# A Conformer-like layer: wg and wu by seven products of quadrants, the ffn in four blocks

## The chip, the cores and the metric

One core of a Trainium2 chip runs the whole layer. The metric is device time in microseconds. Engines in play: PE (TensorE, matmuls; PEld is its loading of weights), DVE (VectorE), ACT (ScalarE), POOL (GpSimd), and SP, which issues the DMAs.

## The reference, cut to what matters

512 tokens, 1024 features, 2816 ffn columns (22 tiles of 128). The layer has a feed-forward (ffn1), a mixer of three attentions, and a second feed-forward (ffn2). Only the two feed-forwards are touched by the change.

```python
def swiglu(h, wg, wu, wd):
    return (jax.nn.silu(h @ wg) * (h @ wu)) @ wd

x = x + 0.5 * swiglu(rmsnorm(x, ffn1_norm[l]), ffn1_wg[l], ffn1_wu[l], ffn1_wd[l])
...
x = x + 0.5 * swiglu(rmsnorm(x, ffn2_norm[l]), ffn2_wg[l], ffn2_wu[l], ffn2_wd[l])
x = rmsnorm(x, final_norm[l])
```

## The kernel before, in words

Every operand of a large product is split into a high and a low part of 12 significant bits (`split`, lines 72 to 75: ACT casts the high part, DVE subtracts it for the low part), and `mm3` (lines 105 to 109) makes three matmuls of each pair: high by high, high by low, low by high.

An ffn (`ffn`, from line 242) first has the normalised tokens in transposed form: `rows_T` and `norm_T` take one tile of 128 tokens at a time, scale it on DVE (line 138), transpose it on PE (line 146) into a PSUM bank `ps_t`, and split it from there into `hh` and `hl` (8 feature tiles by 512 tokens). For each of the 22 tiles of ffn columns, 128 columns of wg and of wu are loaded (`wraw`, 512 KB each), split into `whi` and `wlo` (128 x 1024), and multiplied: 8 feature tiles, three matmuls each, 512 tokens wide (`up_mm`). The gate's bank goes through silu on ACT (line 261), DVE multiplies it with the up product (line 263, tile `pr`), and the result is split into `gh` and `gl`. The first two tiles of each ffn take the tokens in two parts of 256, since the norms of the later tokens are not there yet.

After 11 tiles, `add_product` (line 200) multiplies `gh`, `gl` with the rows of wd in two halves of 512 output columns and adds to `x_sb` on DVE (line 230); then the other 11 tiles follow. Chunks of weights rotate through 5 raw buffers (line 70) and 4 split ones (line 98). In the mixer an order for PE is written out by hand; elsewhere a scheduler orders each engine's instructions by its own estimate of time. ffn2's tokens come from the product with w_out, row tile by row tile (`row_ffn`, tile `norms`).

## Time and profile before

| | us |
|---|---|
| median of 3 runs | 1302.09 (1301.76 to 1302.15) |
| span of the profiled execution | 1299.5 |
| PE busy in it | 1284.3 (99%) |
| DVE busy | 591.0 (45%) |
| ACT busy | 476.7 (37%) |
| POOL busy | 105.3 (8%) |

ffn1 lies from the start to about 390 us, ffn2 from about 920 us to the end. A busy PE only says that some matmul was under way; what one costs is read from the distance between the starts of two.

### The profile page before, as it was taken

The page shows a single profiled execution, that of the slowest core. Times are in us where ns is not written, and L with a number is a line of the kernel's source. Part 1 is how long each engine was busy: PE and PEld are TensorE (multiplying, and loading weights), DVE is VectorE, ACT ScalarE, POOL GpSimd, SP SyncE. Part 2 cuts the span into 40 slices and gives each one's busy share as a digit, 9 for nine tenths or more (in the row PEclk, how much of TensorE's full clock was granted, in tenths as well). Part 3 has the DMA queues.
Part 4 walks back from the last instruction along what each step waited for, and adds up shares of the span by engine and source line. Part 5 has one row for each costly group of instructions (what it writes and reads, how often), then busy time and mean ns, then how long its engine had stood idle before and what let it go on. Part 6 is the DMA issues. An engine that isn't in the chain of part 4 may idle for free.

```text
span 1299.5 us, 16334 instructions
## 1 busy us (share of the span) xinstructions
PE 1284.3 (99%) x6416; PEld 1089.5 (84%) x6416; DVE 591.0 (45%) x1067; ACT 476.7 (37%) x923; POOL 105.3 (8%) x110
## 2 busy tenths in 40 slices
PE   8999999999999999999999999999999999999997
PEld 7888888888888799999999998888888888888886
DVE  5433324333256666766666465454433322333322
ACT  4422213222234446554555454342332211322222
POOL 2000000000000201111122021110000000000010
PEclk8999999999999999999999999999999999999999
DMA  7432233222254403221232121264133223332221
GB/s 266 127 98 89 85 102 113 91 89 89 73 178 139 116 25 107 85 85 50 85 102 75 52 86 49 74 202 162 31 116 98 79 84 97 114 98 90 81 73 65
DMA packets 53132, 127.35 MB, mean 98 GB/s; under 512 B 10176, under 2 KB 10688, under 8 KB 53056
## 3 DMA queue, kind: packets, MB, share of 16 engines
q1 hardware_dynamic: 52480, 125.27, 30.3%
q8 instruction: 50, 0.82, 0.3%
q10 hardware_dynamic: 576, 1.05, 0.2%
q14 instruction: 26, 0.21, 0.1%
HBM read 122.11 MB, written 4.19 MB: 97 GB/s over the span
## 4 chain that ended last, share of the span: by engine, by line
PE 97%; ACT 1%; DVE 1%; DMA 0%; issue 0%; POOL 0%; SPq 0%; POOLq 0%; ACTq 0%; DVEq 0%
PE ps_g L107 12%; PE ps_g L108 12%; PE ps_g L109 12%; PE ps_s L109 7%; PE ps_s L108 7%; PE ps_s L107 7%; PE ps_p L107 7%; PE ps_p L109 7%; PE ps_p L108 7%; PE ps_o L109 3%; PE ps_o L108 3%; PE ps_o L107 3%; PE ps_o L641 2%; PE ps_s L609 2%; PE ps_t L457 1%; PE ps_t L146 1%
## 5 line engine op out<-in xcount | busy, mean ns | idle before, releaser
L74 ACT CAST whi<-wraw 128x1024 fp32r<-128x1024 f32 (+2 forms) x176 | 173.5, 991 | 508.2 <-issue 180.8
L75 DVE TENSOR_TENSOR wlo<-wraw,whi 128x1024 fp32r<-128x1024 f32 (+1 forms) x174 | 199.7, 1151 | 293.8 <-ACT whi L74 288.1
L107 PE MATMUL ps_g<-hh,whi 128*128 128x512 f32 (+1 forms) x288 | 106.4, 370 | 0.8 <-ACT hh L74 0.8
L108 PE MATMUL ps_g<-hl,whi 128*128 128x512 f32 (+1 forms) x288 | 106.6, 370 | 0.0
L109 PE MATMUL ps_g<-hh,wlo 128*128 128x512 f32 (+1 forms) x288 | 106.4, 370 | 0.0
L107 PE MATMUL ps_p<-whi,hh 128*128 128x384 f32 (+1 forms) x264 | 95.2, 360 | 0.0
L107 PE MATMUL ps_s<-hh,whi 128*128 128x512 f32 (+1 forms) x240 | 92.2, 384 | 0.0
L108 PE MATMUL ps_s<-hl,whi 128*128 128x512 f32 (+1 forms) x240 | 92.1, 384 | 0.0
L109 PE MATMUL ps_s<-hh,wlo 128*128 128x512 f32 (+1 forms) x240 | 91.6, 382 | 0.0
L109 PE MATMUL ps_p<-whi,hl 128*128 128x384 f32 (+1 forms) x264 | 89.5, 339 | 0.0
L108 PE MATMUL ps_p<-wlo,hh 128*128 128x384 f32 (+1 forms) x264 | 89.4, 339 | 0.0
L107 PE MATMUL ps_g<-hh,fh 128*128 128x512 f32 x192 | 77.9, 406 | 0.0
L109 PE MATMUL ps_g<-hh,fl 128*128 128x512 f32 x192 | 75.1, 391 | 0.0
L108 PE MATMUL ps_g<-hl,fh 128*128 128x512 f32 x192 | 75.0, 391 | 0.0
L118 POOL TENSOR_TENSOR rsh<-msh,mhalf 128x4 f32<-128x4 f32 x38 | 42.9, 1129 | 262.3 <-DVE msh L124 202.8
L107 PEld LDWEIGHTS ps_g<-hh,whi 128*128 128x128 f32 x288 | 54.1, 188 | 10.9 <-ACT hh L74 1.0
L108 PEld LDWEIGHTS ps_g<-hl,whi 128*128 128x128 f32 x288 | 54.2, 188 | 9.9
L109 PEld LDWEIGHTS ps_g<-hh,wlo 128*128 128x128 f32 x288 | 54.2, 188 | 9.9
L75 DVE TENSOR_TENSOR fl<-wraw,fh 128x768 fp32r<-128x768 f32 x48 | 48.8, 1017 | 26.3 <-ACT fh L74 26.2
L108 PEld LDWEIGHTS ps_s<-hl,whi 128*128 128x128 f32 x240 | 45.8, 191 | 9.4 <-DVE hl L75 0.2
L107 PEld LDWEIGHTS ps_s<-hh,whi 128*128 128x128 f32 x240 | 46.0, 192 | 9.1
L74 ACT CAST fh<-wraw 128x768 fp32r<-128x768 f32 x48 | 39.8, 832 | 37.1 <-PE ps_g L108 22.0
(294 smaller groups left out, 2783.3 us busy)
## 6 DMA issues: line engine op xcount, KB each, us to landing
wraw<-in_ffn_w SPq DMA_DIRECT2D x88, 512.0 KB, 3.5
wraw<-in_ffn_wd SPq DMA_DIRECT2D x40, 512.0 KB, 3.6
wraw<-in_w_u SPq DMA_DIRECT2D x32, 384.0 KB, 3.1
wraw<-in_w_gb SPq DMA_DIRECT2D x32, 384.0 KB, 3.1
wraw<-in_w_gf SPq DMA_DIRECT2D x16, 384.0 KB, 3.1
wraw<-in_w_mem_kv SPq DMA_DIRECT2D x8, 512.0 KB, 4.8
wraw<-in_w_out SPq DMA_DIRECT2D x8, 512.0 KB, 4.1
x_sb<-in_x SPq DMA_DIRECT2D x4, 512.0 KB, 7.1
```

Source lines behind the costliest of these rows:

```text
L74: nc.scalar.copy(out=hi, in_=raw)
L75: (engine or nc.vector).tensor_tensor(out=lo, in0=raw, in1=f32(hi), op=ALU.subtract)
L107: nc.tensor.matmul(ps, lhsT=st[0], rhs=mv[0], start=first, stop=False)
L108: nc.tensor.matmul(ps, lhsT=st[0], rhs=mv[1], start=False, stop=False)
L109: return nc.tensor.matmul(ps, lhsT=st[1], rhs=mv[0], start=False, stop=last)
L118: nc.gpsimd.tensor_tensor(out=rs, in0=ms, in1=mhalf[:, :n], op=ALU.pow)
L146: nc.tensor.transpose(ps[:, k * P:(k + 1) * P], xn[:, c:c + P], ident)
L457: nc.tensor.transpose(ps[:, j * P:(j + 1) * P], pt[:, j * P:(j + 1) * P], ident)
L609: nc.tensor.matmul(out_, lhsT=q, rhs=k, start=j == 0, stop=j == 1)
L641: nc.tensor.matmul(o[:, vs], lhsT=pT[:, j * P:(j + 1) * P], rhs=un.v[:, j, vs], start=j == 0, stop=j == i)
```

## The change

Both operands of h wg and h wu are cut into quadrants: the features into two halves of 512, the tokens into two halves of 256, and the ffn columns into pairs of tiles. The product of such a pair, 2 x 2 quadrants by 2 x 2, is made by seven products instead of eight (Winograd's form of Strassen's method), each half as many tokens wide.

- On the side of the tokens seven operands M1 to M7 (`mhi`, `mlo`) are made once for each ffn. With r0, r1 the two halves of the features and lo, hi the tokens' halves: M1 = r0 lo, M2 = r1 lo, M3 = r1 hi, M5 = t1 = r0 hi - r0 lo, M6 = t2 = r1 hi - t1, M7 = t3 = r1 hi - r0 hi, M4 = t4 = r1 lo - t2. The transposed rows are first copied by ACT into raw tiles; the differences and the splits follow (`Operands`).
- On the side of the weights each pair of tiles (`Item`) loads four raw chunks, as before, which are now quadrants with wg and wu side by side. Four sums s1 to s4 (tiles `quarter`) are made on DVE, and seven blocks are split instead of four: `whi`/`wlo` and, in the feed-forward's own pool, `fhi`/`flo`, a ring of six.
- One product is 24 matmuls of 256 columns (`mm7`): gate and up, four feature tiles, three terms. Products 1, 6, 7 and 4 accumulate in one bank, which ACT copies out between them (`snap`); products 5 and 3 in another; DVE adds the copies (`plus`) and the gating works on halves of the tokens (`gated`).
- The ffn goes in four blocks of 4, 6, 6 and 6 tiles, each followed by its part of the product with wd; a list of jobs gives PE's order, and weights are prepared up to six blocks ahead. The first four products of an ffn need only the first two token tiles.
- Raw buffers become 6. The memory rows' norm is issued before ffn1's last half product instead of between its halves; pools move from the mixer's to one that lasts longer.

Comments were removed as well. The core of the diff, empty lines left out:

```diff
+CHUNKS = (4, 6, 6, 6)
+HS = S // 2
...
-        return base.tile([P, 1024], F32, tag="raw", name=name, bufs=5)
+        return base.tile([P, 1024], F32, tag="raw", name=name, bufs=6)
...
+    def new_M(pool):
+        mh, ml = (pool.tile([P, 7, 4, HS], F32R, name=n) for n in ("mhi", "mlo"))
+        return {i: (mh[:, i - 1], ml[:, i - 1]) for i in range(1, 8)}
+    quarters = [0]
+    def quarter():
+        quarters[0] += 1
+        return base.tile([P, 1024], F32, tag=("w4", "kx")[quarters[0] % 2], name="quarter", bufs=2)
...
+        def rows(self, src, ss, gain, t):
+            ms = tiny("ms", 1)
+            nc.vector.tensor_scalar(out=ms, in0=ss[:, 0:1], scalar1=EPS, scalar2=ss[:, 1:2], op0=ALU.add, op1=ALU.add)
+            rs = rsqrt(ms)
+            xn = scratch("xn")
+            for dh in range(2):
+                norm_half(xn, src, rs, gain, dh)
+                ps = bank("t")
+                for k in range(4):
+                    c = (dh * 4 + k) * P
+                    nc.tensor.transpose(ps[:, k * P:(k + 1) * P], xn[:, c:c + P], ident)
+                nc.scalar.copy(out=self.raw[dh][:, :, t * P:(t + 1) * P], in_=k4(ps))
+            self.combine(t)
+        def combine(self, t):
+            M, (r0, r1) = self.M, self.raw
+            sub = nc.vector.tensor_tensor
+            cols, first = slice(t * P, (t + 1) * P), slice(t % 2 * P, (t % 2 + 1) * P)
+            def part(i, raw, c):
+                split(raw, M[i][0][:, :, c], M[i][1][:, :, c])
+            if t < 2:
+                part(1, r0[:, :, cols], cols)
+                part(2, r1[:, :, cols], cols)
+                return
+            if t == 2:
+                self.t1, self.t2 = k4(quarter()), k4(quarter())
+            t1, t2 = self.t1, self.t2
+            sub(out=t1[:, :, first], in0=r0[:, :, cols], in1=r0[:, :, first], op=ALU.subtract)
+            sub(out=t2[:, :, first], in0=r1[:, :, cols], in1=t1[:, :, first], op=ALU.subtract)
+            part(6, t2[:, :, first], first)
+            if t == 3:
+                lo, hi = slice(0, HS), slice(HS, S)
+                split(t1, *M[5])
+                t3, t4 = k4(quarter()), k4(quarter())
+                sub(out=t3, in0=r1[:, :, hi], in1=r0[:, :, hi], op=ALU.subtract)
+                split(t3, *M[7])
+                sub(out=t4, in0=r1[:, :, lo], in1=t2, op=ALU.subtract)
+                split(t4, *M[4])
+                split(r1[:, :, hi], *M[3])
...
+    def run_jobs(jobs, ring):
+        made = alive = 0
+        for n, job in enumerate(jobs):
+            while made < len(jobs) and (made <= n or alive + jobs[made].blocks <= ring):
+                alive += jobs[made].blocks
+                jobs[made].got = jobs[made].prep() if jobs[made].prep else None
+                made += 1
+            with tc.manual_schedule(engines={mybir.EngineType.PE}):
+                job.run(job.got)
+            alive -= job.blocks
...
-        hh, hl = h
-        nf = NF // 2
-                def up_mm(ps, w, c0, c1):
-                    for k in range(ND):
-                        o = slice(k * P, (k + 1) * P)
-                        mm3(ps[:, c0:c1], (w[0][:, o], w[1][:, o]), (hh[:, k, c0:c1], hl[:, k, c0:c1]),
-                            k == 0, k == ND - 1)
...
-                    # the first tiles take the tokens in two parts, as their norms come in
-                    for c0, c1 in [(0, 256), (256, 512)] if group == 2 else [(0, 512)]:
-                        for i in range(group):
-                            for j in range(2):
-                                up_mm(pss[i][j], ws[i][j], c0, c1)
...
+        RING = 6
+        spot = [0]
+        def block(raw):
+            spot[0] += 1
+            if spot[0] % RING < 4:
+                return weight(None, 1024, raw=raw)
+            return weight(None, 1024, fp, ("fhi", "flo"), RING - 4, raw=raw)
+        def mm7(ps, blk, m, first):
+            for j in range(2):
+                c = slice(j * HS, (j + 1) * HS)
+                for k in range(4):
+                    o = slice((j * 4 + k) * P, (j * 4 + k + 1) * P)
+                    st, mv = tuple(w[:, o] for w in blk), tuple(v[:, k, :] for v in M[m])
+                    for n, (x, y) in enumerate(((st[0], mv[0]), (st[0], mv[1]), (st[1], mv[0]))):
+                        nc.tensor.matmul(ps[:, c], lhsT=x, rhs=y, start=first and j + k + n == 0,
+                                         stop=k == 3 and n == 2, skip_group_check=True)
...
+            def prep(self, p):
+                add = nc.vector.tensor_tensor
+                if p == 1:
+                    return block(self.raw(0))
+                if p == 2:
+                    return block(self.raw(1))
+                if p == 6:
+                    self.s1, self.s2 = quarter(), quarter()
+                    add(out=self.s1, in0=self.raw(2), in1=self.raw(3), op=ALU.add)
+                    add(out=self.s2, in0=self.s1, in1=self.raw(0), op=ALU.subtract)
+                    return block(self.s2)
+                if p == 5:
+                    got = block(self.s1)
+                    self.s4 = quarter()
+                    add(out=self.s4, in0=self.raw(1), in1=self.s2, op=ALU.subtract)
+                    return got
+                if p == 7:
+                    s3 = quarter()
+                    add(out=s3, in0=self.raw(0), in1=self.raw(2), op=ALU.subtract)
+                    return block(s3)
+                if p == 4:
+                    return block(self.raw(3))
+                return block(self.s4)
...
+            def run(self, p, blk):
+                if p == 1:
+                    self.y = bank("s")
+                    mm7(self.y, blk, 1, True)
+                    self.p1 = self.snap()
+                elif p == 2:
+                    x = bank("g")
+                    mm7(x, blk, 2, True)
+                    self.gated(self.plus(x, self.p1), 0, 0)
+                elif p == 6:
+                    mm7(self.y, blk, 6, False)
+                    self.u2 = self.snap()
+                elif p == 5:
+                    self.z = bank("p" if self.ft // 2 % 2 else "o")
+                    mm7(self.z, blk, 5, True)
+                elif p == 7:
+                    mm7(self.y, blk, 7, False)
+                    self.u3 = self.snap()
+                    self.gated(self.plus(self.z, self.u3), 1, 1)
+                elif p == 4:
+                    mm7(self.y, blk, 4, False)
+                    self.gated(self.y, 1, 0)
+                    self.done(1)
+                else:
+                    mm7(self.z, blk, 3, False)
+                    self.gated(self.plus(self.z, self.u2), 0, 1)
+                    self.done(0)
...
+            order = []
+            if ft == 0:
+                order += [(items[0], 1), (items[0], 2), (items[1], 1), (items[1], 2)]
+            else:
+                order += [(items[0], 1), (items[0], 2)]
+            for i, item in enumerate(items):
+                order += [(item, 6), (item, 5), (item, 7)]
+                if i + 1 < len(items) and not (ft == 0 and i == 0):
+                    order += [(items[i + 1], 1)]
+                if ft == 0 and i == 0:
+                    order += [(item, 4), (item, 3)]
+                elif i + 1 < len(items):
+                    order += [(item, 4), (item, 3), (items[i + 1], 2)]
+            jobs = [product(*o) for o in order]
+            end = [product(items[-1], 4), product(items[-1], 3)]
...
+                    for k in range(0, nf, 2):
+                        jobs.append(Job(lambda k=k, chunk=chunk: chunk(k), lambda wc, k=k, run=run: run(wc, k)))
+                        if dh == 0 and k == 0:
+                            jobs += end
...
+    ops = Operands(M1, new_G_as_raw(fp))
+    for t in range(NT):
+        ops.rows(x_sb[:, t, :], squares(x_sb[:, t, :]), gain1, t)
...
+    Mp = right_pool("M2")
+    rawp = right_pool("raw2")
+    M2 = new_M(Mp.__enter__())
+    rp = rawp.__enter__()
+    ops = Operands(M2, [rp.tile([P, 4, S], F32, name=n) for n in ("raw0", "raw1")])
...
-        w = w.reshape(2, ND, P, NF, P).transpose(3, 0, 2, 1, 4)       # ft, g/u, p, k, f
+        w = np.stack([f[pre + "_wg"][0], f[pre + "_wu"][0]])
+        w = w.reshape(2, 2, 4, P, NF, P).transpose(4, 1, 3, 0, 2, 5)
```

How instructions stand in the rows. On PE, inside an ffn, before, where the product for wg (bank `ps_p`) ends and that for wu (bank `ps_o`) begins:

```order
L108 MATMUL ps_p<-hl,whi 128x512
L109 MATMUL ps_p<-hh,wlo 128x512
L107 MATMUL ps_o<-hh,whi 128x512
L108 MATMUL ps_o<-hl,whi 128x512
L109 MATMUL ps_o<-hh,wlo 128x512
```

And now, where product 5 (bank `ps_o`) is broken off for product 6 (bank `ps_s`):

```order
L354 MATMUL ps_o<-mlo,fhi 128x256
L354 MATMUL ps_o<-mhi,flo 128x256
L354 MATMUL ps_o<-mhi,fhi 128x256
L354 MATMUL ps_s<-mhi,whi 128x256
L354 MATMUL ps_s<-mlo,whi 128x256
L354 MATMUL ps_s<-mhi,wlo 128x256
```

The triples of terms stay, with 256 columns in place of 512, and seven groups of 24 stand for two tiles where four groups of 24 stood.

On DVE at the start of ffn1, before, after the norms of the token tiles (`hl` is the low part of the transposed rows, `mt` a row tile of the memory, `wlo` that of a weight chunk, `pr` the first gated product):

```order
L75 TENSOR_TENSOR wlo<-wraw,whi 128x1024
L75 TENSOR_TENSOR hl<-ps_t,hh 128x4x128 x4
L153 TENSOR_SCALAR ms<-ss 128x1
L138 SCALAR_TENSOR_TENSOR xn<-mt,rs,gain 128x512 x2
L75 TENSOR_TENSOR wlo<-wraw,whi 128x1024
L263 TENSOR_TENSOR pr<-sg,ps_s 128x512
```

And now, where the last operands M are made (`gl` is here the memory of r1; L379 makes s1, L380 s2, L402 is `plus`), up to the low part of s1's block:

```order
L78 TENSOR_TENSOR mlo<-gl,mhi 128x1024
L413 TENSOR_TENSOR pr<-sg,cc 128x256
L78 TENSOR_TENSOR mlo<-quarter,mhi 128x4x128
L379 TENSOR_TENSOR quarter<-wraw 128x1024
L78 TENSOR_TENSOR mlo<-quarter,mhi 128x1024
L141 SCALAR_TENSOR_TENSOR xn<-mt,rs,gain 128x512
L402 TENSOR_TENSOR cc<-ps_g,snap 128x512
L141 SCALAR_TENSOR_TENSOR xn<-mt,rs,gain 128x512
L78 TENSOR_TENSOR mlo<-quarter,mhi 128x1024
L380 TENSOR_TENSOR quarter<-quarter,wraw 128x1024
L78 TENSOR_TENSOR wlo<-quarter,whi 128x1024
```

The fifth product's block (the last row) now stands behind the splits of M3 to M7, two of the memory's half norms and the first additions.

On DVE at the start of ffn2, before, around the fourth row tile's norm (`norms`):

```order
L75 TENSOR_TENSOR wlo<-wraw,whi 128x1024
L75 TENSOR_TENSOR hl<-ps_t,hh 128x4x128
L153 TENSOR_SCALAR ms<-sst 128x1
L75 TENSOR_TENSOR hl<-ps_t,hh 128x4x128
L138 SCALAR_TENSOR_TENSOR norms<-x_sb,rs,norms 128x512 x2
L75 TENSOR_TENSOR hl<-ps_t,hh 128x4x128 x4
```

And now, from the first piece of the fourth row's t1 (L220) to the low part of the fourth product's block (`flo<-wraw`); L227 is t3, L229 t4:

```order
L220 TENSOR_TENSOR quarter<-raw_9396 128x4x128
L227 TENSOR_TENSOR quarter<-raw_9397,raw_9396 128x1024
L221 TENSOR_TENSOR quarter<-raw_9397,quarter 128x4x128
L78 TENSOR_TENSOR mlo<-raw_9397,mhi 128x1024
L229 TENSOR_TENSOR quarter<-raw_9397,quarter 128x1024
L78 TENSOR_TENSOR mlo<-quarter,mhi 128x1024 x2
L78 TENSOR_TENSOR mlo<-quarter,mhi 128x4x128
L78 TENSOR_TENSOR mlo<-quarter,mhi 128x1024
L379 TENSOR_TENSOR quarter<-wraw 128x1024
L78 TENSOR_TENSOR flo<-wraw,fhi 128x1024
```

Four splits of 512 columns followed the fourth norm before; now all of these stand ahead of the fourth product's block.

## Rows read from the trace of the kernel before

**Rows 1.** The page: span, PE's busy time, and the chain that ended last by engine.
```profile
span 1299.5 us, 16334 instructions
...
PE 1284.3 (99%) x6416; PEld 1089.5 (84%) x6416; DVE 591.0 (45%) x1067; ACT 476.7 (37%) x923; POOL 105.3 (8%) x110
...
PE 97%; ACT 1%; DVE 1%; DMA 0%; issue 0%; POOL 0%; SPq 0%; POOLq 0%; ACTq 0%; DVEq 0%
```

**Rows 2.** Busy time by stretch: engines' us (instructions), granted clock, DMA share, GB/s.
```profile
13.00:20.00 7.00, 6.37 (x33) 5.57 (x32) 6.04 (x6) 5.65 (x11) 4.99 (x4) 0.63 0.87 325
20.00:40.00 20.00, 20.00 (x171) 20.00 (x170) 10.86 (x16) 8.49 (x14) 0.99 (x2) 1.00 0.50 170
50.00:70.00 20.00, 20.00 (x87) 16.21 (x87) 6.26 (x7) 5.63 (x7) 0.00 (x0) 1.00 0.36 107
...
220.00:250.00 30.00, 30.00 (x130) 24.32 (x130) 8.85 (x10) 8.24 (x11) 0.00 (x0) 1.00 0.31 103
```

**Rows 3.** Groups by line: one form of matmul, and one group of weight loads.
```profile
L107 PE MATMUL ps_g<-hh,whi 128*128 128x512 f32 x224 | 88.4, 395 | 0.0
...
L107 PEld LDWEIGHTS ps_g<-hh,whi 128*128 128x128 f32 x288 | 54.1, 188 | 10.9 <-ACT hh L74 1.0
```

**Rows 4.** Timeline of PE, start and duration in us.
```profile
13.30 0.56 PE L107 MATMUL ps_s<-hh,whi 128*128 128x256 f32 x1
...
14.54 0.41 PE L107 MATMUL ps_s<-hh,whi 128*128 128x256 f32 x1
...
16.46 0.41 PE L107 MATMUL ps_s<-hh,whi 128*128 128x256 f32 x1
...
28.76 0.28 PE L107 MATMUL ps_g<-hh,whi 128*128 128x256 f32 x1
...
34.81 0.28 PE L107 MATMUL ps_s<-hh,whi 128*128 128x256 f32 x1
...
60.04 0.39 PE L107 MATMUL ps_s<-hh,whi 128*128 128x512 f32 x1
...
69.80 0.39 PE L107 MATMUL ps_g<-hh,whi 128*128 128x512 f32 x1
```

**Rows 5.** Groups of DVE and ACT by line and form: busy us, mean ns of one.
```profile
L75 DVE TENSOR_TENSOR wlo<-wraw,whi 128x1024 fp32r<-128x1024 f32 x134 | 163.6, 1225 | 253.0 <-ACT whi L74 247.9
...
L75 DVE TENSOR_TENSOR gl<-pr,gh 128x512 fp32r<-128x512 f32 x44 | 30.1, 684 | 0.0
...
L574 DVE TENSOR_TENSOR y<-ps_p,gb 128x256 f32<-128x256 f32 x16 | 6.6, 415 | 0.0
...
L74 ACT CAST whi<-wraw 128x1024 fp32r<-128x1024 f32 x136 | 141.7, 1049 | 457.0 <-issue 178.3 <-PE ps_g L108 66.8 <-PE ps_s L109 56.0
...
L74 ACT CAST gh<-pr 128x512 fp32r<-128x512 f32 x44 | 27.3, 621 | 0.1
...
L459 ACT COPY pT<-ps_t 128x512 f32<-128x512 f32 x20 | 11.3, 590 | 24.0 <-PE ps_t L457 24.0
```

**Rows 6.** Timeline of DVE at the start of ffn1, to its fourth gated tile.
```profile
6.58 1.41 DVE L138 SCALAR_TENSOR_TENSOR xn<-x_sb,rs,gain 128x512 f32<-128x512 f32 x2 [0.75 <-POOL rs L118]
...
10.48 1.40 DVE L138 SCALAR_TENSOR_TENSOR xn<-x_sb,rs,gain 128x512 f32<-128x512 f32 x2
...
21.81 1.22 DVE L75 TENSOR_TENSOR wlo<-wraw,whi 128x1024 fp32r<-128x1024 f32 x1
22.94 1.28 DVE L75 TENSOR_TENSOR hl<-ps_t,hh 128x512 fp32r<-128x512 f32 x2
...
63.79 0.69 DVE L263 TENSOR_TENSOR pr<-sg,ps_s 128x512 f32<-128x512 f32 x1 [3.52 <-PE ps_s L109]
```

**Rows 7.** Timeline of DVE at the start of ffn2, to its fourth gated tile.
```profile
917.14 1.42 DVE L138 SCALAR_TENSOR_TENSOR norms<-x_sb,rs,norms 128x512 f32<-128x512 f32 x2 [0.66 <-POOL rs L118]
918.58 0.69 DVE L230 SCALAR_TENSOR_TENSOR x_sb<-ps_s,x_sb 128x512 f32<-128x512 f32 x1
...
968.34 0.69 DVE L263 TENSOR_TENSOR pr<-sg,ps_g 128x512 f32<-128x512 f32 x1 [3.55 <-PE ps_g L109]
```

More of the change, by code (lines that the diff above doesn't have):

```diff
@@ L161, in rows_T, with squares @@
+    def squares(src):
         ss = tiny("ss", 2)
@@ L242, in ffn, with __init__ @@
-    def ffn(pre, x_sb, h, after, between=None, raws=None, after_half=None):
+                add_rows(x_sb, acc[t], t, dh, scale, after)
+    class Job:
+        def __init__(self, prep, run, blocks=1):
+            self.prep, self.run, self.blocks = prep, run, blocks
+    def run_jobs(jobs, ring):
[8 more added lines that the diff above has]
+            alive -= job.blocks
@@ L297, in layer_kernel @@
-    mT = [mem_pool.tile([P, ND, NM], F32R, name=n) for n in ("mh", "ml")]
-    def mem_rows():
+        RING = 6
[14 more added lines that the diff above has]
+                                         stop=k == 3 and n == 2, skip_group_check=True)
@@ new lines, in new_G_as_raw @@
+    def new_G_as_raw(fp):
+        return [fp.tile([P, 6, S], F32R, tag=t, name=t).bitcast(F32)[:, 0:4, :] for t in ("gh", "gl")]
+    fpool = tc.tile_pool(name="ffn1", bufs=1, reuse_waits="tile")
+    fp = fpool.__enter__()
+    ops = Operands(M1, new_G_as_raw(fp))
+    for t in range(NT):
+        ops.rows(x_sb[:, t, :], squares(x_sb[:, t, :]), gain1, t)
+    mix_in = {}
+    def mem_rows():
+        Mp.__exit__(None, None, None)
+        mix_in["h2p"] = right_pool("h2p")
+        p = mix_in["h2p"].__enter__()
+        mix_in["h"] = tuple(p.tile([P, ND, S], F32R, name=n) for n in ("hh", "hl"))
+        mix_in["mTp"] = right_pool("mTp")
+        p = mix_in["mTp"].__enter__()
+        mix_in["mT"] = [p.tile([P, ND, NM], F32R, name=n) for n in ("mh", "ml")]
@@ L303, in mem_rows @@
             nc.sync.dma_start(out=mt, in_=a["mem"][t * P:(t + 1) * P, :])
-            rows_T(mt, gain, mT, t)
-    h1 = new_hT()
-    for t in range(NT):
-        rows_T(x_sb[:, t, :], gain1, h1, t)
-    mix_in = {}
+            norm_T(mt, squares(mt), gain, mix_in["mT"], t)
     def row_mix(t, ss):
@@ L314, in row_mix @@
             mix_in["g"] = load_gain("mix_norm")
-            mix_in["h"] = new_hT()
         norm_T(x_sb[:, t, :], ss, mix_in["g"], mix_in["h"], t)
         nc.sync.dma_start(out=x_dram[t * P:(t + 1) * P, :], in_=x_sb[:, t, :])
-    ffn("ffn1", x_sb, h1, row_mix, between=mem_rows, raws=w1_raw)
-    h2 = mix_in["h"]
+    ffn("ffn1", x_sb, M1, fp, row_mix, raws=w1_raw, before_last=mem_rows)
+    h2, mT = mix_in["h"], mix_in["mT"]
+    fpool.__exit__(None, None, None)
+    memp.__exit__(None, None, None)
+    memp = tc.tile_pool(name="memw", bufs=1, reuse_waits="tile")
+    mem_pool = memp.__enter__()
     def heads(ap, n):
@@ L753, in y_done @@
         if d == 4:
-            yT.append([mp.tile([P, 4, S], F32R, tag="qk", name=n, bufs=2) for n in ("yh", "yl")])
+            yT.append([mo.tile([P, 4, S], F32R, tag="qk", name=n, bufs=2) for n in ("yh", "yl")])
         yh, yl = (v[:, d % 4, :] for v in yT[d // 4])
@@ L787, in row_ffn @@
         if t == 0:
-            parts = [mp.tile([P, NT, 512], F32, tag=tag, name="norms", bufs=2) for tag in ("oh", "ol")]
+            parts = [mo.tile([P, NT, 512], F32, tag=tag, name="norms", bufs=2) for tag in ("oh", "ol")]
             parts = [v.rearrange("p a b -> p (a b)")[:, o:o + 1024] for v in parts for o in (0, 1024)]
@@ L818, in row_out @@
         nc.scalar.dma_start(out=out[t * P:(t + 1) * P, 512:], in_=xn[:, 512:])
-    ffn("ffn2", x_sb, ffn_in["h"], row_out, after_half=row_half)
+    ffn("ffn2", x_sb, M2, fp, row_out, after_half=row_half)
+    fpool.__exit__(None, None, None)
+    Mp.__exit__(None, None, None)
 def _rope_table():
```

177 lines of the change are left out of this document (114 added, 63 removed).

## The prediction, made before the changed kernel ran

> **What bounds the kernel now.** I read the page first: TensorE (PE) is busy 99% of the span and the chain that ended last is 97% PE [rows 1]. So a gain must take time off PE's own queue, and any other engine matters only where PE starts to wait for it. Then the busy time by stretches [rows 2]: in the feed-forward stages PE is full, at the full clock (1.00, the 2.4 GHz level), with VectorE (DVE) at about 30% (8.85 of 30 us) and ScalarE (ACT) about the same. A busy PE says nothing about the cost of one matmul, so I take the pitch, start to start, from the timeline [rows 4]: with 512 columns, 42 matmuls from 60.04 to 69.80 us, 0.2324 us each; with 256 columns, 51 matmuls from 28.76 to 34.81 us, 0.1186 us each. Half the columns cost 51% of the time: this decides the case, and it is measured in the very operation that changes. The same timeline at the lower clock (1.2 GHz), from 14.54 to 16.46 us, gives 0.213 us for 256 columns.
>
> **Part 1: what the seven products save.** Before, an ffn has 22 feature tiles x 2 (gate, up) x 8 x 3 = 1056 matmuls for wg and wu; two tiles of each ffn take 256 columns (192 matmuls), the rest are 960 with 512; [rows 3] is the largest of four groups of leading terms, 640 in all, a third of 2 x 960. That is 960 x 0.2324 + 192 x 0.1186 = 245.9 us. After: 11 pairs of tiles x 7 products x 24 = 1848 matmuls of 256 columns, x 0.1186 = 219.2 us. Saved: 26.7 us an ffn, 53.4 us in all, if PE never waits. The product with wd keeps its 1056 matmuls of 512 columns an ffn; four blocks instead of two halves add only drains of PSUM (16 more adds of 512 columns an ffn), beside PE.
>
> **Part 2: what VectorE and ScalarE get.** A pair of tiles had four weight blocks to split; now seven, and four sums of 1024 columns, three additions of a saved PSUM bank (512), four gatings (256) and two splits (512). VectorE by durations [rows 5]: 11 x 1.225 + 3 x 0.69 + 4 x 0.415 + 2 x 0.684 = 18.6 us a pair; PE needs 168 x 0.1186 = 19.9 us. Back to back it is less, since the next instruction starts before the last has left: 21.81 to 22.94 us is 1.13 us for the 1024 columns [rows 6], and so about 0.61 for 512: some 16.8 us a pair. The Trainium skill ("VectorE: DVE Perf Modes", The DRAIN you can't avoid) says that the next instruction doesn't start until the pipeline is empty; the trace shows 0.09 us of overlap there; by the rule the pair would cost the full 18.6 us and each start about 2 us more. ScalarE: 7 x 1.05 + 3 x 0.59 + 4 x 0.39 + 2 x 0.62 = 11.9 us (0.39 for 256 columns is an estimate between the rows). So VectorE is 84 to 93% full among the pairs, but the wd product of three pairs, 288 x 0.2324 = 66.9 us of PE, asks it only for 6 splits and 8 adds (13 us), and up to six blocks can be made ahead (14 us of PE). In mid-stage I therefore expect no steady wait. Its price from both sides: no gain is possible, as PE is already full, so 0; and 0.5 us a pair for the 18 later pairs, 9 us, if a snapshot of the bank comes late. The order puts another product (2.85 us) between a snapshot and the next product into that bank, and ScalarE needs 0.59 us and a 1.05 us split ahead of it; only in each ffn's first pair do products 7 and 4 follow each other directly. I take 2 us in all, near the lower end.
>
> **Part 3: the start of ffn1.** Here everything comes at once on VectorE. PE: the first product needs both parts of the first two token tiles. Before, matmuls began at 13.3 us with the high part alone, much of it at the low clock [rows 2, 4]; in the new order four casts of M1 and M2, two splits of weights and the third tile's norm stand ahead, and I get 18.1 us. The four products that need only M1 and M2 then take 16 matmuls x 0.213 + 80 x 0.1186 + 8 transposes (about 1 us) = 13.9 us: PE is through at 32. The next needs the block of s1, whose VectorE split stands in the queue behind all the new operands: 10 half norms (two of them of mem, now early) x 0.66, four splits of weights x 1.13, ten pieces of 512 x 0.61, nine of 1024 (t3, t4, four splits of M, s1, s2, and the block) x 1.13, two additions and small ones (2.0): 29.4 us, from 6.58 us, with some 3.5 us of waits for the second and third tile of x (the second's norm starts at 10.48 now) and 1 to 2 us of hand-overs [rows 6]: 41 us. PE waits some 9 us, comes back at the low clock (16 matmuls x 0.095 = 1.5 us) and has ten products left (28.5 us) and one late snapshot (1 us): its first four tiles are done at 72 us, without the wd product that slips in. Before, at 63.79 us [rows 6]. **ffn1 loses 8.4 us here**, and gains 864 x 0.2324 - 1512 x 0.1186 = 21.5 us on the 18 other tiles: **-13.1 us**.
>
> **Part 4: the start of ffn2.** The third row's norm is at 917.14 and the fourth row's add at 918.58 us [rows 7]; up to there nothing changes on PE. After: the first product starts when the third row's transposes and the second's splits are through, 921.3; three products and the last transposes take 9.6 us: 930.9. The fourth needs its block's low part, which the new order puts behind all of the fourth row's operands: from 922.4, norm 1.3, five pieces of 512 (3.1), six of 1024 (6.8), one more of 512, s1 and the block (2.3), and waits for ScalarE's copies of the fourth row (about 1): 937.4 us, PE waits 6.5. Then each block is made just before its use: product 5 at 941.5 (1.3 lost), 6 and 7 to 949.8, 2 us for the next pair's s2, and the rest without a gap: 972.4 us. Before, at 968.34 [rows 7]. **It loses 4.1 us, gains 21.5: -17.4 us.**
>
> **Sum.** 1299.5 - 13.1 - 17.4 + 2 = 1271.0 us of span; the median of the runs lies 2.6 us over the span: **1273.6 us**. The attention between the two (400 to 900 us) has the same matmuls; its pools move but its two queues of weights stay. The last rows are as before: one row's matmuls, add, norm, store.
>
> **Rivals.** (a) The starts are hidden: VectorE's list is shorter, or PE finds other work. Then nearly all of 53.4 us comes: 1299.5 - 53.4 + 2 + 2.6 = 1251 us, with half the start costs (the first four tiles should save 5.2 us, so 13.6 and 9.3 us) 1262. For it: the operands of the first products exist early. Against: 29 us of VectorE work by measured durations, in an order that is fixed. 0.13. (b) VectorE also paces the middle a little: 0.5 us a pair and 8% more at both starts (18.6 for 16.8): 1273.6 + 7 + 5 = 1286 us. For it: 93%. Against: the six blocks ahead. 0.13. (c) Slower than before: VectorE becomes the bound among the pairs. With about 9 us of work ahead at a block's start and 59.8 us of PE for three pairs, it binds from (59.8 + 9)/3 = 22.9 us a pair, and eats the 28.5 us of gain over six blocks at (59.8 + 9 + 4.8)/3 = 24.5 us; at 25 us a pair the time is some 1311. It would take a third more than the durations. 0.04. (d) The matmuls of half length don't take half the time, as each needs its own load of weights. The row of weight loads is full in the 256-column stretch (20.00 of 20 us) and not in the other (16.21) [rows 2]; were the load's 0.188 us [rows 3] the floor instead of 0.1186, 3696 x 0.069 = 257 us would be added, and the time be about 1530. The Trainium skill ("TensorE: Matmul & The Clock Gate", Part 3, The mechanism) has such a rule: a load overlaps with running matmuls only when the row groups differ, and here they don't. The pitch of 0.1186 us, just over the stream of 256 columns, contradicts it. 0.01.
>
> **How the numbers follow.** The forecast, 1262 to 1283, has 0.69. The range of 8 in 10 takes half of (a) and most of (b): 1259 to 1287. A measurement tells about 0.2%, 2.6 us, from no change. Faster by more: 0.94 (forecast, a, b); slower by more: 0.04 (c, d and a rest); within: 0.02.
>
> **What would show it.** In the new profile: a pitch of 0.119 us for matmuls of line 354; VectorE full from 12 to 45 us and PE with one gap of about 9 us near 32 to 41; a gap of about 6 us near the start of ffn2; PE full, VectorE at 80 to 90%, in stretches of pairs; seven tenths of ScalarE at most. Wrong if the pitch is over 0.13 us beside the fuller VectorE, if PE shows short waits for VectorE or for snapshots in every pair, or if the gaps at the starts are absent.

## The result, and the profile after

The changed kernel takes **1273.12 us** (median, 1272.50 to 1273.49) against 1301.92 us of the kernel before beside it: a ratio of 0.978 (95% interval 0.977 to 0.980). The forecast was 1273.6 us. That is nearer than the steps deserve: two of them were wrong, by about the same amount and in opposite directions, and only a comparison stage by stage shows it.

The page of the changed kernel: span, PE's busy time (the number after the x is that of instructions) and the chain that ended last.

```profile
span 1271.3 us, 19657 instructions
...
PE 1232.4 (97%) x7808; PEld 1116.9 (88%) x7808; DVE 842.8 (66%) x1377; ACT 596.8 (47%) x1115; POOL 107.1 (8%) x108
...
PE 90%; DVE 4%; DMA 2%; ACT 1%; POOL 1%; issue 1%; SPq 0%; POOLq 0%; ACTq 0%; DVEq 0%
```

PE still sets the end, but its share of the chain fell from 97% [rows 1] to 90%: DVE and DMA now hold stretches of it. To see where, I cut the span at two adds that both kernels have. They are the last add of ffn1 and the last of w_out, on DVE's timeline (start, duration in us). The kernel before, then the one after:

```profile
392.11 0.69 DVE L230 SCALAR_TENSOR_TENSOR x_sb<-ps_o,x_sb 128x512 f32<-128x512 f32 x1
...
918.58 0.69 DVE L230 SCALAR_TENSOR_TENSOR x_sb<-ps_s,x_sb 128x512 f32<-128x512 f32 x1
```

```profile
374.52 0.68 DVE L271 SCALAR_TENSOR_TENSOR x_sb<-ps_g,x_sb 128x512 f32<-128x512 f32 x1
...
911.74 0.69 DVE L271 SCALAR_TENSOR_TENSOR x_sb<-ps_s,x_sb 128x512 f32<-128x512 f32 x1
```

| stretch | before, us | after, us | change | forecast |
|---|---|---|---|---|
| start to the end of ffn1 | 392.1 | 374.5 | -17.6 | -13.1 |
| attention and w_out | 526.5 | 537.2 | **+10.7** | 0 |
| ffn2 to the end | 380.9 | 359.6 | -21.4 | -17.4 |
| waits of PE behind the first four tiles (forecast: in mid-stage) | | in the rows above | +1.7, inside those rows | +2 |

Both ffns gained some 4 us more than forecast, and the attention, where no arithmetic changed, lost 10.7.

**The attention's entry.** Busy time by stretch after (columns as in [rows 2]), and the same stretches before:

```profile
405.00:410.00 5.00, 3.40 (x15) 2.42 (x13) 3.57 (x4) 4.05 (x5) 0.00 (x0) 1.00 0.52 163
410.00:415.00 5.00, 1.02 (x3) 0.87 (x4) 4.09 (x8) 1.87 (x4) 1.65 (x1) 0.77 0.93 297
415.00:420.00 5.00, 5.00 (x16) 3.92 (x15) 3.60 (x9) 0.65 (x2) 2.74 (x3) 0.55 0.04 16
```

```profile
405.00:410.00 5.00, 5.00 (x28) 4.21 (x27) 3.69 (x5) 3.38 (x6) 1.01 (x1) 1.00 0.28 82
410.00:415.00 5.00, 5.00 (x23) 4.08 (x22) 3.84 (x8) 0.38 (x1) 1.01 (x1) 1.00 0.21 79
415.00:420.00 5.00, 5.00 (x28) 4.10 (x27) 2.55 (x4) 2.16 (x3) 0.00 (x0) 1.00 0.12 30
```

Before, PE is full there. After, it stands for 5.6 us and then works 5 us at a granted clock of 0.55, near the 1.2 GHz level: 16 matmuls where 28 fitted. PE's timeline names what it waited for:

```profile
413.98 0.76 PE L110 MATMUL ps_s<-mwh,mh 128*128 128x512 f32 x1 [5.57 <-DVE mk L580]
```

This is the first matmul of the memory's values (`mv`). Its two "s" banks still hold the memory's keys (`mk`), which DVE reads last in their norm at line 580. Before, the product of the memory's queries (`cq`) lay between keys and values and covered that norm. In the new order the queries come first, since the keys' weights now go into a pool that opens only when ffn1's pool has closed; nothing is left to put between. ScalarE's timeline agrees: the first cast of the keys' weights (`mwh`) was at 362.4 us before, 30 us ahead of ffn1's last add, and comes 13 us behind it now:

```profile
387.86 2.00 ACT L77 CAST mwh<-wraw 128x1024 fp32r<-128x1024 f32 x2
```

**The pitch.** PE's timeline in mid-stage, the first and the last of 24 matmuls with weights from the ring's base part (`whi`, `wlo`), then of 23 with weights from its ffn part (`fhi`, `flo`):

```profile
117.83 0.28 PE L354 MATMUL ps_o<-mhi,whi 128*128 128x256 f32 x1
...
120.44 0.28 PE L354 MATMUL ps_o<-mhi,wlo 128*128 128x256 f32 x1
120.56 0.28 PE L354 MATMUL ps_s<-mhi,fhi 128*128 128x256 f32 x1
...
123.20 0.28 PE L354 MATMUL ps_s<-mlo,fhi 128*128 128x256 f32 x1
```

2.61 us over 23 steps is 0.1135 us; 2.64 over 22 is 0.1200. The forecast took 0.1186 for all, from the kernel before [rows 4]. With four blocks of the ring in six in the base part the mean is 0.1157 us.

**The starts** came as forecast. PE's timeline in ffn1 (the bracket is the idle time before, and what ended it), with the end of the first four tiles there and in ffn2:

```profile
34.66 0.58 PE L354 MATMUL ps_o<-mhi,whi 128*128 128x256 f32 x1 [3.64 <-ACT whi L77]
...
40.47 0.58 PE L354 MATMUL ps_s<-mhi,fhi 128*128 128x256 f32 x1 [2.17 <-ACT fhi L77]
...
77.38 0.28 PE L354 MATMUL ps_p<-mhi,wlo 128*128 128x256 f32 x1
...
971.14 0.28 PE L354 MATMUL ps_p<-mhi,wlo 128*128 128x256 f32 x1
```

PE runs dry at 31.0 us and goes on at 40.5, with two matmuls and eight transposes at the low clock between: the 9 us gap of the forecast (32 to 41). The bracket names ScalarE's cast of s2, but that cast waited for VectorE's sum s2, and the low part of s1's block ends with the gap, at 39.25 + 1.22 = 40.47 us. DVE's timeline there:

```profile
38.12 1.22 DVE L380 TENSOR_TENSOR quarter<-quarter,wraw 128x1024 f32<-128x1024 f32 x1
39.25 1.22 DVE L78 TENSOR_TENSOR wlo<-quarter,whi 128x1024 fp32r<-128x1024 f32 x1
```

DVE is busy for 31.25 of the 33 us from 12 to 45. In ffn2 PE stands for 2.96 and 3.69 us, up to 926.4 and 930.6 us. A piece of the wd product, 5.8 us, lies inside the first four tiles; without it they end at 77.4 + 0.3 - 5.8 = 71.9 us, forecast 72. In ffn2, set back by the 6.8 us by which w_out ended earlier and without its wd piece (5.6 us), 971.1 + 0.3 + 6.8 - 5.6 = 972.6, forecast 972.4. Among the later pairs PE never waits, with DVE at 86%:

```profile
113.00:143.00 30.00, 30.00 (x261) 30.00 (x261) 25.82 (x31) 18.07 (x28) 0.00 (x0) 1.00 0.28 88
```

But behind the first four tiles of each ffn, PE waits once for their last gated rows (`gh`), 1.65 us in all:

```profile
81.53 0.50 PE L110 MATMUL ps_g<-fhi,gh 128*128 128x512 f32 x1 [0.59 <-ACT gh L77]
...
975.30 0.50 PE L110 MATMUL ps_g<-fhi,gh 128*128 128x512 f32 x1 [1.06 <-ACT gh L77]
```

### The profile page after: what moved, and what is told of

It is laid out like the page before. It is cut to its first block, busy times and chain, and to the rows that moved or that the text cites. A ratio compares the mean times of both kernels' runs of the same rounds, so it can differ in the third digit from the quotient of the medians.

```text
span 1271.3 us, 19657 instructions
## 1 busy us (share of the span) xinstructions
PE 1232.4 (97%) x7808; PEld 1116.9 (88%) x7808; DVE 842.8 (66%) x1377; ACT 596.8 (47%) x1115; POOL 107.1 (8%) x108
## 4 chain that ended last, share of the span: by engine, by line
PE 90%; DVE 4%; DMA 2%; ACT 1%; POOL 1%; issue 1%; SPq 0%; POOLq 0%; ACTq 0%; DVEq 0%
PE ps_s L354 19%; PE ps_g L110 9%; PE ps_g L112 9%; PE ps_g L111 9%; PE ps_o L354 5%; PE ps_p L110 4%; PE ps_p L354 4%; PE ps_p L111 4%; PE ps_p L112 4%; PE ps_g L354 4%; PE ps_s L110 2%; PE ps_s L112 2%; PE ps_s L111 2%; PE ps_o L881 2%; PE ps_s L849 2%; PE ps_t L697 1%
## 5 line engine op out<-in xcount | busy, mean ns | idle before, releaser
L77 ACT CAST whi<-wraw 128x1024 fp32r<-128x1024 f32 (+1 forms) x120 | 119.0, 993 | 141.3 <-PE ps_s L354 68.6
L78 DVE TENSOR_TENSOR wlo<-wraw,whi 128x1024 fp32r<-128x1024 f32 (+1 forms) x120 | 137.9, 1151 | 65.6 <-ACT whi L77 64.6
L354 PE MATMUL ps_s<-mhi,whi 128*128 128x256 f32 x496 | 138.3, 279 | 2.3 <-ACT snap L397 2.0
L354 PE MATMUL ps_s<-mlo,whi 128*128 128x256 f32 x496 | 137.7, 278 | 0.0
L354 PE MATMUL ps_s<-mhi,wlo 128*128 128x256 f32 x496 | 136.8, 278 | 0.0
L354 PEld LDWEIGHTS ps_s<-mhi,whi 128*128 128x128 f32 x496 | 93.8, 189 | 4.1 <-ACT snap L397 2.8
L354 PEld LDWEIGHTS ps_s<-mlo,whi 128*128 128x128 f32 x496 | 93.7, 189 | 1.0 <-DVE mlo L78 0.2
L354 PEld LDWEIGHTS ps_s<-mhi,wlo 128*128 128x128 f32 x496 | 93.2, 189 | 0.0
L78 DVE TENSOR_TENSOR wlo<-quarter,whi 128x1024 fp32r<-128x1024 f32 x54 | 65.9, 1221 | 24.5 <-ACT whi L77 24.5
L77 ACT CAST fhi<-quarter 128x1024 fp32r<-128x1024 f32 x34 | 35.5, 1049 | 59.1 <-PE ps_s L354 16.4
L354 PE MATMUL ps_s<-mhi,fhi 128*128 128x256 f32 x208 | 59.2, 285 | 2.5 <-ACT fhi L77 2.5
```

The costliest lines, as they stand in the source:

```text
L77: nc.scalar.copy(out=hi, in_=raw)
L78: (engine or nc.vector).tensor_tensor(out=lo, in0=raw, in1=f32(hi), op=ALU.subtract)
L354: nc.tensor.matmul(ps[:, c], lhsT=x, rhs=y, start=first and j + k + n == 0, stop=k == 3 and n == 2, skip_group_check=True)
```

## The experiments

The kernel before, run again beside each change, took 1300.95 to 1301.92 us, so a difference of about 1 us between two experiments says nothing.

**1. Half length without seven products.** The kernel before, all its wg and wu matmuls in halves:

```diff
-                    for c0, c1 in [(0, 256), (256, 512)] if group == 2 else [(0, 512)]:
+                    for c0, c1 in [(0, 256), (256, 512)]:
```

> The kernel before with all products with wg and wu in two halves of 256 columns (as it has them for its first two tiles only): half length without the seven products. Theory 1, by the pitches of the kernel before (0.1186 and 0.2324 us): 1920 matmuls become 3840, 1920 x (2 x 0.1186 - 0.2324) = 9.2 us more, 1311 us. Theory 2, the pitch of 0.1135 us that most matmuls of the changed kernel show belongs to the half length itself in a steady stage: 1920 x (2 x 0.1135 - 0.2324) = 10.4 us less, 1291.5 us.

Measured: 1310.55 us against 1300.95 us before, 1.0076 (1.0061 to 1.0091): +9.6 us. Its pitch in mid-stage is 0.1187 us, so it isn't half length that made 0.1135. Theory 1: half length alone costs what the forecast's working says, and the gain of the change comes from the smaller number of products in spite of it.

**2. What sets the pitch.** The places of the operands in the partitions differ between the two parts of the ring, so I let TensorE run alone on chosen addresses. The core of the three kernels of this kind (one large tile `big`, `at` gives the address in it):

```python
for w, wl, m, ml in COMBOS:          # weights, distance to their low part, columns, the same
    ...
    for n, (x, y) in enumerate(((0, 0), (0, ml), (wl, 0))):
        nc.tensor.matmul(ps[:, c], lhsT=at(w + x + o, 128), rhs=at(m + y + mv, 256), ...)
```

> TensorE alone: 26 sets of 48 matmuls of 256 columns, with a new weight load each and in the order of the seven products (high x high, high x low, low x high), out of one large tile; nothing else of the layer is computed. Each set takes its weights and its moving columns from chosen addresses of a partition; three sets are the addresses of the changed kernel (weights of the ring's base part, of its ffn part, of the gated rows), two those of the kernel before. Theory 1, the places of the two operands set the pitch: 113.5 ns for the base part (59936) against 172000 and 120.0 ns for the ffn part (131136) against 172000, as in the changed kernel, and about 118.6 ns for 72224 against 39072, as in the kernel before; shifts by 32 or 64 bytes then tell whether it is the alignment. Theory 2, the difference comes from what the other engines read and write meanwhile: all sets take 113.5 ns here.

The three levels appear with all other engines idle: sets at 113.5, at about 117.6 and at 120.0 ns. So it isn't traffic (theory 2 falls). But the base part's addresses showed 117.6 ns at their first place in the run and 113.5 at their last, so theory 1 isn't the whole of it.

> As m_addr, TensorE alone and all in a written order: 42 sets of 48 matmuls of 256 columns out of one tile, after everything is filled; nothing of the layer is computed. Ten sets have the base part's addresses of the changed kernel (59936, 172000), three of them in one PSUM bank and one in each of the others; eight have the ffn part's (131136, 172000), one in each bank; sixteen take the weights at 59904 + 0, 32, 64, 96 and the columns at 172032 + 0, 32, 64, 96; eight change the distance between high and low parts, or are the other pairs of the two kernels and the first again. Theory 1, the two addresses set the pitch (113.5, about 118 or 120 ns): the ten sets agree among themselves and the eight too, and the sixteen fall into groups by the difference modulo 128. Theory 2, the PSUM bank, or the state in which a stretch begins, sets it: equal addresses show different pitches, by bank or without a rule.

PE's timeline of m_addr2 inside three sets: the base part's addresses, the ffn part's, and those of the kernel before. A row gathers n matmuls; its duration less the last one's 0.28 us, over n - 1, is the pitch.

```profile
59.75 3.45 PE L87 MATMUL bank<-big 128*128 128x256 f32 x29
...
99.31 3.40 PE L87 MATMUL bank<-big 128*128 128x256 f32 x27
...
241.27 3.49 PE L87 MATMUL bank<-big 128*128 128x256 f32 x28
```

0.1132, 0.1200 and 0.1189 us: the three pitches of the two kernels (0.1135, 0.1200, 0.1186), out of nothing but addresses. The base part's ten sets agree (the first left out, whose first matmuls start 0.21 us apart, the pitch of the lower clock), the ffn part's eight too, whatever the PSUM bank; changing the distance between high and low parts by 8192 or 12288 bytes does nothing. The difference modulo 128 alone does not order the sixteen sets.

> TensorE alone, nothing of the layer: 64 sets of 48 matmuls of 256 columns with the weights at 59904 + 0, 32 ... 224 and the columns at 172032 + 0, 32 ... 224 bytes of a partition, then 8 sets of 48 matmuls of 512 columns as those of wd, with the weights at 94208 + 0, 32 ... 224 and the columns at 59936. Theory 1, the place of both modulo 256 sets the pitch: the pairs (32, 224) and (64, 0), the one of the changed kernel's base part and one found beside it, take 113.5 ns, the ffn part's pair (64, 224) 120 ns, and the 512-column sets show 227 ns at some offsets and 232 at the others. Theory 2, more than 256 bytes of the address count, or the state in which a set begins: the pair (64, 224) is not at 120.0 or (32, 224) not at 113.5 ns here.

The table of 64 pairs runs along its diagonals: the distance from weights to columns modulo 256 counts, not the two places, except that at 160 and 192 pairs of one distance take two values. In ns (the row of 512 columns has one set for each distance):

| distance | 0 | 32 | 64 | 96 | 128 | 160 | 192 | 224 |
|---|---|---|---|---|---|---|---|---|
| 256 columns | 119.9 | 117.8 | 117.8 | 119.8 | 118.7 | 117.4 or 118.6 | 113.4 or 117.7 | 118.3 |
| 512 columns | 226.8 | 233.1 | 228.9 | 233.3 | 232.5 | 234.3 | 233.3 | 233.3 |

Three sets of m_addr3 with the distance 192 or 160: the pair (32, 224), (64, 224) and (96, 32).

```profile
112.26 3.46 PE L82 MATMUL bank<-big 128*128 128x256 f32 x28
...
157.77 3.49 PE L82 MATMUL bank<-big 128*128 128x256 f32 x28
...
169.27 3.45 PE L82 MATMUL bank<-big 128*128 128x256 f32 x29
```

That is 0.1178, 0.1189 and 0.1132 us. The first is the base part's pair, at 0.1132 in m_addr2; the second the ffn part's, at 0.1200 there. So at two distances the pitch has more than one value, and theory 2 is right there: the stretch before plays a part. What chooses stays open.

**3. The same in the whole kernel.** An unused tile at the front of each ffn's pool moves the ffn part and the gated rows; the instructions stay.

```diff
     fp = fpool.__enter__()
+    fp.tile([P, 8], F32, name="pad")        # e_pad32;  [P, 56] in e_pad224
```

> The changed kernel with one unused tile of 32 bytes at the front of each ffn's pool, so that the ffn part of the ring of split weights and the gated rows lie 32 bytes further on; the instructions are the same. Theory 1, the alignment of the operands sets the pitch: the 1232 matmuls with ffn-part weights go from 120.0 to 113.5 ns, 8.0 us less, 1265 us, and the matmuls of wd may change by up to 5 ns each way. Theory 2, alignment is not it (distance, half of the memory, or traffic): 1273 within 2 us.

Measured: 1274.73 us (0.980 of before, 0.978 to 0.982). The ffn part's matmuls came down to 118.4 ns on average, as the table has it for distance 128, but a part of the base part's, whose addresses were not touched, went up to 117.8 (mean 114.7 for 113.8). By the total this is theory 2, and alignment alone isn't the rule: the matmuls that theory 1 sent to 113.5 ns went to 118.4.

> The changed kernel with one unused tile of 224 bytes at the front of each ffn's pool; same instructions in the same order. The ffn part of the ring and the gated rows then lie at 32 modulo 256 as the base part does: the distance from weights to columns modulo 256 is 192 for all products of the seven (the pair that takes 113.5 ns) and 0 for all of wd (226.8 ns in m_addr3). Theory 1, that distance sets the pitch in the whole kernel as in the sets alone: 1232 x 6.5 ns = 8.0 us and 2112 x 2/3 x 5.6 ns = 7.9 us less, 1273.1 - 16 = 1257 us (1255 to 1261). Theory 2, the 192 distance falls into its slower value (117.7 ns, as some stretches of e_pad32 did): 3696 x 2.2 ns = 8 us more than that, 1265 us. Theory 3, places are without effect in the whole kernel: 1273 within 2 us.

Measured: 1274.43 us (0.979, 0.978 to 0.981). wd's matmuls take 226.9 ns for 233.2, as the table says. But with the distance at 192 everywhere, nearly all of the seven products' matmuls settled at the slower of its two values: 117.2 ns on average, for 113.8 and 119.8. 2496 x 3.4 - 1200 x 2.6 ns = +5.4 us, and 720 x 6.3 + 336 x 1.1 = -4.9 us for wd: 0.5 us more, measured 1.3. The slower value is theory 2's, but its 1265 us is missed by 9: both sums count 2112 matmuls of wd where there are 1056 in the two ffns, and theory 2 adds 2.2 ns a matmul where 117.2 is 3.7 above the 113.5 hoped for. With both put right it is 1273.1 - 8.0 - 3.9 + 13.7 = 1274.9 us. The total lies within theory 3's 2 us, and yet places have their effect: the two effects cancel.

**4. The attention's entry.** Keys, then queries, then values, the keys' weights in the base ring:

```diff
-    mk_ps = rows_product([bank("s") for _ in range(NMT)], mT, a["w_mem_kv"], 0, **mem_w)
+    with tc.manual_schedule(engines={mybir.EngineType.PE}):
+        mk_ps = rows_product([bank("s") for _ in range(NMT)], mT, a["w_mem_kv"], 0)
+        cq_ps = rows_product([bank(t) for t in ("p", "g", "g", "o")], h2, a["w_in"], 3072)
     for t in range(NMT):
...
-    cq_ps = rows_product([bank(t) for t in ("p", "g", "g", "o")], h2, a["w_in"], 3072)
```

> The changed kernel with the memory's keys ahead of the memory's queries on TensorE, in the order as written, and with the keys' weights in the ring of the base pool instead of the pool that opens after ffn1; the values stay last. Theory 1, the loss of 10.7 us between the end of ffn1 and w_out is the order of these three products (the values wait for the keys' norm, 5.6 us at 414 us, and then run at half the clock until 420): both go, 1273.1 - 8 = 1265 us (1263 to 1267). Theory 2, the loss lies in the attention's later steps or in ScalarE's casts: within 2 us of 1273.1.

Measured: 1263.62 us, 0.971 (0.970 to 0.973): 9.5 us less than the changed kernel. In its trace the two adds stand so:

```profile
374.63 0.68 DVE L271 SCALAR_TENSOR_TENSOR x_sb<-ps_g,x_sb 128x512 f32<-128x512 f32 x1
...
902.09 0.68 DVE L271 SCALAR_TENSOR_TENSOR x_sb<-ps_s,x_sb 128x512 f32<-128x512 f32 x1
```

and PE is full between 405 and 420 us:

```profile
410.00:415.00 5.00, 5.00 (x24) 4.08 (x23) 5.00 (x10) 1.85 (x4) 1.83 (x2) 1.00 0.41 105
```

ffn1 ends where it did; the attention takes 527.5 us for 537.2, before 526.5. So 9.7 of the 10.7 us went with the order of the three products. The run changes the order and the keys' pool together; that the pool turned the order is read from the program and the casts, not tested by itself. The 1.0 us left fits the pitches in that stage (an estimate): 864 matmuls of the gates take 232.1 ns for 229.1, 768 of the projections 173.5 for 175.3, which makes +1.2 us.

**5. What paces the starts.** Taking work off DVE's list by giving it to GpSimd, in e_mix2:

```diff
-                split(t1, *M[5])
+                split(t1, *M[5], engine=nc.gpsimd)       # and M[7], M[4], M[3]
```

> The kernel of e_mix2 with the low parts of the operands M5, M7, M4 and M3 made by GpSimd instead of VectorE, at both ffns' starts: 4 x 1.13 = 4.5 us less on VectorE ahead of the fifth product's block in ffn1 and the fourth's in ffn2, and 4 x 2.6 = 10.3 us on GpSimd, idle there. Theory 1, VectorE's list sets the gap at each start: each shrinks by 3 to 4.5 us, 1263.6 - 7 = 1256.5 us (1255 to 1259). Theory 2, TensorE waits there for ScalarE (casts, copies of the transposed rows, snapshots): within 2 us of 1263.6. Theory 3, GpSimd is too slow or slows VectorE: M5 to M3 come late and the time is over 1265.6.

Measured: 1275.63 us, 0.980 (0.979 to 0.982): 12 us slower than e_mix2, theory 3. DVE's timeline in e_pool at the start of ffn1, and GpSimd's:

```profile
27.29 1.22 DVE L227 TENSOR_TENSOR quarter<-gl,gh 128x1024 f32<-128x1024 f32 x1
28.42 3.45 DVE L229 TENSOR_TENSOR quarter<-gl,quarter 128x1024 f32<-128x1024 f32 x1
...
34.89 3.35 DVE L379 TENSOR_TENSOR quarter<-wraw 128x1024 f32<-128x1024 f32 x1
38.17 0.68 DVE L402 TENSOR_TENSOR cc<-ps_g,snap 128x512 f32<-128x512 f32 x1
```

```profile
28.11 2.69 POOL L78 TENSOR_TENSOR mlo<-quarter,mhi 128x1024 fp32r<-128x1024 f32 x1 [7.87 <-ACT mhi L77]
30.75 3.32 POOL L78 TENSOR_TENSOR mlo<-gl,mhi 128x1024 fp32r<-128x1024 f32 x1
...
34.74 5.74 POOL L78 TENSOR_TENSOR mlo<-quarter,mhi 128x1024 fp32r<-128x1024 f32 x2
```

A sum of 1024 columns takes 1.22 us on DVE, and 3.45 when GpSimd began 0.3 us ahead of it: it ends 1.07 us after GpSimd's instruction does. The addition with one operand in PSUM (38.17) is not held up. That is the rule of the Trainium skill ("SBUF — State Buffer", Who interferes with whom): an instruction of VectorE with two inputs in SBUF and one of GpSimd that reads SBUF exclude each other, and the second waits out the first. The rows agree. PE's wait in ffn1 grew with DVE's list, from 4.4 to 7.7 us (the chief one), which fits a DVE that paces the start.

Then the order, again in e_mix2: M7, M4 and M3 made only with the blocks of their own products.

```diff
             def prep(self, p):
                 add = nc.vector.tensor_tensor
+                late.pop(p, lambda: None)()      # 7: t3, M7, t4;  4: M4;  3: M3
```

> The kernel of e_mix2 with the operands M7, M4 and M3 made only when the blocks of products 7, 4 and 3 are, so that on VectorE the blocks of s2 and s1 stand ahead of them; t3 and t4 are made in place. Same work. Up to the last input of the waiting product VectorE's list is shorter by two to five instructions of 1024 columns (2.3 to 5.7 us) at each start. Theory 1, this list sets the gaps: each shrinks by 2 to 5 us, 1263.6 - 7 = 1256.5 us (1253.5 to 1260). Theory 2, the products behind then wait for the later operands instead, and the gap only moves: within 2 us of 1263.6.

Measured: 1260.89 us, 0.969 (0.967 to 0.970), 2.7 us less where theory 1 asked for 7; partly theory 2. In the profiled runs ffn2 took 2.3 us less than in e_mix2 (356.6 for 359.0), but ffn1 ended 1.7 us later (last add at 376.38 for 374.63; the profiled run of e_late is 1.5 us above its median). There PE went on earlier and then stood again, among others for the memory's transposes, which had come early (timeline of PE, e_late):

```profile
33.66 0.47 PE L357 MATMUL ps_s<-mhi,fhi 128*128 128x256 f32 x1 [1.85 <-ACT mhi L77]
35.93 1.94 PE L149 MATMUL ps_t<-ident,xn 128*128 128x128 f32 x8 [1.80 <-DVE xn L141]
38.23 0.58 PE L357 MATMUL ps_o<-mlo,whi 128*128 128x256 f32 x1 [0.36 <-DVE mlo L78]
```

**6. Together.** e_best is e_late with the 224 bytes; e_best2 moves the attention's tiles too.

```diff
         mix_in["h"] = tuple(p.tile([P, ND, S], F32R, name=n) for n in ("hh", "hl"))
+        p.tile([P, 48], F32, name="pad")
...
     mp = mix.__enter__()
+    mp.tile([P, 32], F32, name="pad")
```

> The kernel of e_late (the keys ahead of the queries, the later operands made late) with the unused 224 bytes of e_pad224. Theory 1, the gains add: 1260.9 - 16 = 1245 us (1243 to 1249). Theory 2, the shorter pitch turns into waits for VectorE in the pairs (7 x 24 x 0.1135 = 19.1 us of TensorE a pair against 16.8 of VectorE): less than 12 us of it arrives, over 1249 us.

Measured: 1262.22 us, 0.970 (0.968 to 0.971), with the pitch of e_pad224 again (117.2 ns): nothing gained on e_late. The 16 us of theory 1 carries e_pad224's double count of wd with it.

> The kernel of e_best with 192 unused bytes behind the attention's input and 128 ahead of the attention's tiles, so that the projections' and the gates' weights and columns have distance 0 modulo 256 too. Theory 1, the 768 matmuls of 384 columns (173.5 ns now) and 576 of 512 (231.5 ns now) come down by 3 to 5 ns each: 4 to 6 us less than e_best, 1240 us. Theory 2, TensorE doesn't set the pace in the attention: within 2 us of e_best.

Measured: 1261.98 us, 0.970 (0.969 to 0.972), within 2 us of e_best. The gates' matmuls came down by 1.5 ns (231.5 to 230.0), the projections' went up by 1.7 (173.5 to 175.2): the expected 3 to 5 ns were not there, so this run doesn't tell whether TensorE sets the pace in the attention.

Last, the memory's norms away from the start, and the distance at 0 for wd's base part only:

```diff
-            mt = scratch("mt")
+            mt = buf4k("mt")
```

> The kernel of e_late with two changes. The memory's row tiles are loaded into the ring of raw weights, so that their norms can't come early: four half norms (2.6 us) leave VectorE's list at the start of ffn1, for the end of ffn1. And the gated rows lie 224 bytes further on, the ffn part of the ring 256: the distance modulo 256 of wd's operands is 0 for the base part of the ring, 32 for the ffn part, while the products of seven keep their 192 and 160. Theory 1, VectorE's list at the start costs TensorE its full length, and the distance its pitch: 2.6 us, and 704 x 5.9 ns less for wd's base part against 352 x 5.5 ns more for the ffn part (2.2 us): 1260.9 - 4.8 = 1256 us (1254 to 1258.5). Theory 2, TensorE's waits at the start have moved to ScalarE and the snapshots, and the two-valued 192 pair goes to 117.7 ns here: 1261 us or more.

Measured: **1256.56 us**, 0.965 (0.964 to 0.967), the fastest of all: 4.3 us less than e_late, as theory 1's sum had it, but not by its terms. wd's base part did take 227.7 ns for 233.2, yet its ffn part 233.6 for 228.0, and a part of the seven products' matmuls fell to the slower value (mean 114.5 for 113.8): 4.0 us less, 1.9 and 1.7 us more, so about nothing, and ffn2 takes the same time as in e_late (356.4 us for 356.6). Nearly all of the gain is in ffn1, whose last add comes at 371.30 us for 376.38, and for 374.63 in e_mix2, so a third of the 5.1 us is what e_late had lost there. The start no longer has eight transposes of the memory on PE, four half norms on DVE and the waits for them. PE's timeline there:

```profile
33.87 0.39 PE L357 MATMUL ps_s<-mhi,fhi 128*128 128x256 f32 x1 [2.17 <-ACT mhi L77]
35.49 0.58 PE L357 MATMUL ps_o<-mlo,whi 128*128 128x256 f32 x1 [1.23 <-DVE mlo L78]
```

PE is back at 35.5 us, where the changed kernel was at 40.5.

## Why the prediction was right, point by point

- **Seven products for eight: right in kind, the pitch mis-sized.** Part 1 took 0.1186 us for every matmul of 256 columns. It is 0.1157 on average in the changed kernel, which makes 1512 x 0.0029 = 4.3 us more on the 18 later tiles of each ffn: -13.1 becomes -17.4 (measured -17.6), -17.4 becomes -21.7 (measured -21.4). The price was read in the right operation, at other addresses.
- **The starts: right** to some tenths of a us in their ends, and in place. DVE's list as their cause is borne out by e_pool, where it grew, by e_late in ffn2, where it was reordered, and by e_best3, where it was cut. In ffn1 e_late alone lost time. In e_best3 more than DVE's own 2.6 us came back, since PE's transposes went with it.
- **Waits in mid-stage: 2 us assumed for late snapshots, none found there.** The 1.65 us for `gh` behind the first four tiles has the same size by luck; no term names it. Nor does any name the product with wd, which was taken as unchanged: its matmuls with weights from the ffn part of the ring take 228.2 ns for 233.3, and 336 of them save 1.7 us. DVE's 86% among pairs was within the forecast 80 to 90%. One number of that part was wrong: three pairs need 144 matmuls of wd and not 288, 33.5 us and not 66.9 (528 an ffn, not 1056). DVE's 13 us there still fit, and no term used it.
- **"The attention between the two has the same matmuls; its pools move but its two queues of weights stay": the step that failed**, by 10.7 us. The order of three products changed, by the program because of the moved pool, and with it went the cover of a norm. It could have been seen before the run, in the new program's order on PE: queries, keys, values for keys, queries, values. The forecast put it at nothing on the counts of matmuls and queues alone.
- **The sum.** 1271.0 - 2 x 4.3 (pitch) - 0.3 (waits of 1.65 for 2) - 1.7 (wd) + 10.7 = 1271.1 us, measured 1271.3. So the seven products work as forecast, and the near hit of the total is luck: the attention's loss and the shorter pitches cancel.
- **Rival (d)** (each half-length matmul bound by its weight load) is out, by e_halves too. (b) and (c), DVE as the pace of the pairs, are out: no later pair waits. (a), the hidden starts, is what e_best3 goes a part of the way to.

## What to carry to other kernels

A change in one stage that moves a pool also moves the first instant at which the next stage's tiles can be written; read the new order at every boundary behind the edit, and for each wait there ask which product used to cover it. Here the order's part is measured, the pool's is read from the program. Price an operation at the addresses that it will have, or keep several ns a matmul as an unknown: with thousands of them that is some us. And a total that comes true is no proof of its terms: cut both traces at shared instructions and compare stretch by stretch.
